# Q and K of a hybrid encoder block: per-head norms taken from the PSUM banks in a written order, eight banks in rotation, K's weight parts prepared under another list of ticks

## The chip, the cores and the metric

One core of one Trainium2 chip. The metric is the device time of one execution in microseconds; the kernel before has a median of 1204.8 us over three runs (1204.0 to 1205.54). All other times here are from one profiled execution of it.

## The reference

One encoder layer on 1024 tokens of width 1024, in float32. What matters here is the projection to Q and K and the norm of each head:

```python
u = rms_norm(x, norm1_g[l])
proj = u @ w_in[l]
q, k, v, cb, cc, ch, ga, gb = jnp.split(proj, split_pts, axis=-1)
q = rms_norm(q.reshape(B, S, N_HEADS, HEAD_DIM), q_norm_g[l])
k = rms_norm(k.reshape(B, S, N_HEADS, HEAD_DIM), k_norm_g[l])
...
y_a = neighbourhood_attention(q, k, v, rpb[l]) @ w_attn_branch[l]
y_b = short_gated_conv(cb, cc, ch, conv_w[l]) @ w_conv_branch[l]
merged = jax.nn.sigmoid(ga) * y_a + jax.nn.sigmoid(gb) * y_b
x = x + merged @ w_o[l]
h = rms_norm(x, norm2_g[l]) @ w_mlp_in[l]
x = x + jnp.square(jax.nn.relu(h)) @ w_mlp_out[l]
```

There are 8 heads of 64, so Q and K are 512 wide each. `rms_norm` divides by the root of the mean square plus 1e-6 and multiplies by a gain.

## The kernel before

Every matmul runs in float16 with both operands split into a high and a low half; three passes (high-high, high-low, low-high) give one product. Splitting is vector work: ScalarE writes the high half, VectorE subtracts it from the float32 value to get the low half. The same is done for the weights, after a scale that comes from the sum of their squares: ScalarE squares the raw weights, TensorE adds over the partitions with a matmul of ones (`all_sum`), VectorE turns the sum into a power of two (`pow2_half`), and then the parts are split. `Chunk.prep` is the generator that emits this for one group of weights.

The tokens are in eight blocks of 128. A unit is one token block against one weight group of 512 columns: 8 slices of the inner dimension by 3 passes, 24 matmuls into one PSUM bank. The stages around the change: V units for blocks 2, 6, 3, 7, 4, 5; eight Q units; eight K units; two units of the first conv group; then the attention stage, in which the conv's other matmuls are mixed with the attention's.

The order of the vector work is set by hand. `fg` and `bg` are lists of generators. `step()` advances all of `fg` by one `yield`, `tick()` the first of `bg`; each call emits a few instructions. `unit(mms, post, steps, ticks)` emits the matmuls, runs the `post` of the unit before (through `settle`), and then interleaves so many steps and ticks. `apart(mark, n)` holds a generator back until n more units have been emitted, and `forced` overrides that. All engines run their instructions in order, so what is emitted earlier on an engine stands in front.

In the Q and K stage each unit's `post` adds a `qk_vec` generator to `fg`: ScalarE copies the bank to `qs` with a scale (L714), squares it (L715); VectorE reduces per head (L718), `rstd` makes the inverse root (VectorE L405, ScalarE's square root L406, VectorE L408 to L414), then VectorE multiplies (L725, for K also the gain, L728), ScalarE makes the high half (L732) and VectorE the low half (L734). `finish_qk` transposes the halves by DMA into `QD` or `KD`. The banks alternate between tag `d` (3 banks) and tag `o` (2 banks).

Beside it run the `sforms`: for four pairs of token blocks, x times its norm (ScalarE L484), four sums on GpSimd (L490), split into halves (ScalarE L504, VectorE L506) and stored to DRAM as `GS` (L511, issued by ScalarE) for a later stage. `xt`, which they read, lies where `QD` is put afterwards. K's weights are prepared by `bg` during the Q units, the first conv group's during the K units. The loop:

```python
for n, (kind, b) in enumerate(todo):
    ch = cQ if kind == "q" else cK
    if n % 8 == 0:
        push(cK if kind == "q" else cConv[0])
    ps = bank("do"[n % 2])
    ...
    unit(tok_mms(ps, actU, b, ch, 8, 512, 0), post, 4, 6 if 4 < n < 8 else 3)
    if n == 3:
        forced[0] = True
        while formed[0] < 4:
            step()
        forced[0] = False
```

Of the kernel before, what the change touches and what calls it, by code (L numbers as in the profile page):

```python
# [10 lines left out]
F32 = mybir.dt.float32  # L11
F16 = mybir.dt.float16
# [40 lines left out]
def encoder_block(ctx: ExitStack, tc: tile.TileContext, x, weights, cols, gqk, rel, masks, out):  # L53
# [22 lines left out]
        return bank("dsodsods"[rc[0] % 8])  # L76


    sc = base.tile([128, 516], F32, name="sc")
    sci = sc.bitcast(I32)  # L80
    area = {"keep": [0, 0, 148], "prep": [148, 148, 244], "tmp": [244, 244, 516]}

    def cols_of(kind, n):
        a = area[kind]
# [6 lines left out]
    def keep(n=1):  # L91
        return cols_of("keep", n)

    def tmp(n=1):
        return cols_of("tmp", n)
# [86 lines left out]
    def apart(mark, n=3, of=units):  # L182
        while of[0] < mark + n and not forced[0]:
            yield WAIT
# [60 lines left out]
    class Chunk:  # L245
# [9 lines left out]
        def prep(self):  # L255
# [5 lines left out]
            if self.kind in "QKCG":  # L261
                self.parts = wsp.tile([128, 2, tot], F16, name="w16_ws", tag="ws")
                for p, (k, w) in enumerate(self.widths):
                    while len(self.raw) <= p:
                        yield WAIT
                    A.activation(self.parts[:, 1, :k * w].bitcast(BF16), self.raw[p][:, :k * w], AF.Square,
                                 accum_out=sc[:, at(rm, p)])
# [4 lines left out]
                V.tensor_tensor(c, sc[:, a], sc[:, gm2], op=OP.mult)  # L272
# [96 lines left out]
    warm = keep()  # L369
    V.memset(sc[:, warm], 1.0)  # L370
    A.activation(sc[:, warm], sc[:, warm], AF.Square)
    minus_half = keep()
    G.memset(sc[:, minus_half], -0.5)
    load_x(0)
    SP.dma_start(sc[:, consts], cols)
# [41 lines left out]
    def rpow(ss, n, y, top):  # L417

        v = tmp()
        G.tensor_scalar(sc[:, v], sc[:, ss], 4.0 ** -top / n, 4.0 ** -top * EPS, op0=OP.mult, op1=OP.add)  # L420
        G.tensor_tensor(sc[:, y], sc[:, v], sc[:, minus_half], op=OP.pow)
        yield

    def pow2_half(ss, top, s, inv, more=0):
# [53 lines left out]
    turned, formed = set(), [0]  # L478
    SFORM = ((9, 0, 0), (9, 2, 1), (10, 1, 0), (10, 3, 1), (11, 0, 1), (12, 1, 1))
# [6 lines left out]
    def sform_sums(n):  # L486
        z = [xt[:, b, c:c + 512] for b in (n, n + 4) for c in (0, 512)]
        for o, a, b, op in ((3, 2, 3, OP.subtract), (2, 0, 2, OP.subtract),
                            (0, 3, 0, OP.subtract), (1, 1, 0, OP.add)):
            G.tensor_tensor(z[o], z[a], z[b], op=op)  # L490

    def sforms():

        for mark, n, split in SFORM:
            yield from apart(mark, 0)
            pair = xt[:, n:n + 5:4]
            if not split:
                sform_rows(n)
                sform_sums(n)
                continue  # L500
            v = wqk.tile([128, 4, 2, 512], F16, name="s16", bufs=3)
            v4 = v.rearrange("p (b h) w c -> p b h w c", b=2)
            f = pair.rearrange("p b (h c) -> p b h c", h=2)
            A.activation(v4[:, :, :, 0], f, AF.Copy)  # L504
            yield
            V.tensor_tensor(v4[:, :, :, 1], f, v4[:, :, :, 0], op=OP.subtract)  # L506
            fg.append(sform_store(n, v))

    def sform_store(n, v):
        yield from apart(units[0], 1)  # L510
        A.dma_start(GS[:, n], v)  # L511
        formed[0] += 1

    def ln_step(b, n=1):
        for _ in range(n):
# [2 lines left out]
    def qk_gain():  # L518
        g = gq[:, 0]
        V.tensor_tensor(g, g, gq[:, 1], op=OP.mult)  # L520
        yield
        yield from gain(g, 11, sgq, isgq)

    def turn_row(b):
        ln_turn(u16[:, ORDER.index(b) % 4], b, UT)
# [164 lines left out]
        ln_step(b, 2)  # L690
        turn_row(b)
    fg.append(qk_gain())
    fg.append(sforms())
    for b in 4, 5:
        v_unit(b, 11)
        step(3)
    settle()
    flush()

    def bias_load(p):  # L700
        t = wbias.tile([128, 2, 3, 128], F32, name="bias")
# [6 lines left out]
        V.scalar_tensor_tensor(te, te, sc[:, cinv], mk[:, 0], op0=OP.mult, op1=OP.add)  # L708
        G.tensor_tensor(m[:, e], te, mk[:, 1], op=OP.add)

    def qk_vec(ps, inv, kind, res):
        qs = wqk.tile([128, 512], F32, name="qs", bufs=3)
        sq = wqk.tile([128, 512], F32, name="sq", bufs=1)
        A.activation(qs, ps, AF.Copy, scale=sc[:, inv])  # L714
        A.activation(sq, qs, AF.Square)  # L715
        yield
        ss, y = tmp(8), tmp(8)
        V.tensor_reduce(sc[:, ss], sq.rearrange("p (h d) -> p h d", h=8), axis=AX, op=OP.add)  # L718
        yield
        yield from rstd(ss, HD, y, 12 if kind == "q" else 0)  # L720
        if kind == "k":
            V.tensor_scalar(sc[:, y], sc[:, y], sc[:, sgq], None, op0=OP.mult)
            yield
        q3 = qs.rearrange("p (h d) -> p h d", h=8)
        V.tensor_tensor(q3, q3, sc[:, y][:, :, None].to_broadcast([128, 8, HD]), op=OP.mult)  # L725
        yield
        if kind == "k":
            V.tensor_tensor(q3, q3, gq[:, 0][:, None, :].to_broadcast([128, 8, HD]), op=OP.mult)  # L728
        r = 2 if kind == "q" else 1
        t = wqk.tile([128, 8, 2, r, HD], F16, name=kind + "16", tag="q16")  # L730
        q4 = q3[:, :, None, :].to_broadcast([128, 8, r, HD])
        A.activation(t[:, :, 0], q4, AF.Copy)  # L732
        yield
        V.tensor_tensor(t[:, :, 1], q4, t[:, :, 0], op=OP.subtract)  # L734
        res.append(t)

    q16 = {}
    todo = [("q", b) for b in ORDER] + [("k", b) for b in range(8)]

    def finish_qk(n):  # L740
        kind, b = todo[n]
        while not q16[n]:
            step()
        dst = QD.rearrange("p a e w t -> p (a e w) t") if kind == "q" else KD
        SP.dma_start_transpose(dst[:, :, b * 128:(b + 1) * 128], q16.pop(n)[0].rearrange("p h w r d -> p (h w r d)"))

    for n, (kind, b) in enumerate(todo):
        ch = cQ if kind == "q" else cK
        if n % 8 == 0:
            push(cK if kind == "q" else cConv[0])  # L750
        ps = bank("do"[n % 2])
        q16[n] = []

        def post(ps=ps, kind=kind, n=n, ch=ch):
            fg.append(qk_vec(ps, ch.inv, kind, q16[n]))
        unit(tok_mms(ps, actU, b, ch, 8, 512, 0), post, 4, 6 if 4 < n < 8 else 3)
        if n == 3:
            forced[0] = True
            while formed[0] < 4:
                step()  # L760
            forced[0] = False
# [8 lines left out]
            SP.dma_start(mk, masks)  # L770
# [4 lines left out]
        if n >= 3:  # L775
            finish_qk(n - 3)
        if n in (5, 6):
            bias_make(*bias[0], n - 5)
        if n % 8 == 7:
            flush()  # L780

# [9 lines left out]

    conv_start(0)
    push(cConv[1])
    first = [bank("o"), bank("o")]
    for half in range(2):
        unit(ch_mms(first[half], actU, half, cConv[0], 8, 384, 0), None, 8, 4)
        finish_qk(13 + half)
    while not q16[15]:
        step()
    settle()  # L800
    finish_qk(15)
    A.activation(sc[:, warm], sc[:, warm], AF.Exp)
    settle()
    drain()
# [1117 lines left out]
```

## Time and profile before

| what | value |
|---|---|
| median of three runs | 1204.8 us |
| the profiled execution | 1205.96 us |
| its span | 1204.2 us |
| TensorE (PE) busy | 1190.9 us, 99% of the span |
| VectorE (DVE) busy | 929.0 us, 77% |
| ScalarE (ACT) busy | 763.3 us, 63% |
| GpSimd (POOL) busy | 435.1 us, 36% |

Times in the views are from the span's start. PEld is TensorE's weight load, which overlaps its matmuls; `ACTq` and `SPq` are the DMA queues that ScalarE and SyncE issue to. The Q units begin at 55.81 us, the K units at 97.28, the conv's first unit at 140.77, and the attention stage at 153.53. Matmuls are pipelined: a unit's matmuls are shown a little longer than the distance from one unit to the next. In brackets stands the idle time ahead of an instruction and what ended it.

### The profile page before, as it was taken

How to read it: one execution, taken by the hardware profiler on the slowest of the kernel's cores; microseconds unless marked ns; L12 is line 12 of the kernel's file. 1: busy time of each engine (PE TensorE's matmuls, PEld its weight loads, DVE VectorE, ACT ScalarE, POOL GpSimd, SP SyncE). 2: the span in 40 equal slices, each digit the busy share in tenths (PEclk: the TensorE clock that was granted, in tenths of full speed). 3: DMA queues.
4: the chain of work that ended last, by engine and by line, in shares of the span. 5: the costliest groups of instructions: out<-in, count | busy, mean ns of one | idle time of the engine just before them, and what ended most of it. 6: DMA issues, size and time to landing. Idle time of an engine off the chain costs nothing.

```text
span 1204.2 us, 16886 instructions
## 1 busy us (share of the span) xinstructions
PE 1190.9 (99%) x6206; PEld 574.7 (48%) x6206; DVE 929.0 (77%) x1721; ACT 763.3 (63%) x1185; POOL 435.1 (36%) x292
## 2 busy tenths in 40 slices
PE   8999999999999999999999999999999999999998
PEld 6444445555444444444468444444444444444444
DVE  6767988988368686877878655545549999999997
ACT  7876679867554555337779778678676744746440
POOL 1641011222311112001004465565567471554662
PEclk9999999999999999999999999999999999999999
DMA  9956746676451211224286545445465926345302
GB/s 284 220 181 139 139 119 134 130 146 120 106 121 68 64 60 52 70 92 188 53 159 185 183 156 192 151 138 193 147 247 201 355 94 223 124 139 194 105 35 105
DMA packets 177250, 174.91 MB, mean 145 GB/s; under 512 B 137744, under 2 KB 138256, under 8 KB 173072
## 3 DMA queue, kind: packets, MB, share of 16 engines
q1 hardware_dynamic: 176592, 169.65, 49.0%
q10 hardware_dynamic: 576, 4.19, 0.8%
q8 instruction: 48, 0.79, 0.3%
q14 instruction: 34, 0.28, 0.1%
HBM read 102.51 MB, written 37.75 MB: 116 GB/s over the span
## 4 chain that ended last, share of the span: by engine, by line
PE 78%; DVE 5%; issue 1%; SPq 1%; ACT 1%; DMA 0%; DVEq 0%; ACTq 0%
PE ps_d L210 28%; PE ps_s L210 24%; PE ps_o L210 17%; PE ps_d L1017 6%; PE ps_o L994 1%; PE ps_s L937 1%; SPq L1088 1%; DVE P L977 1%; DVE w_s L1141 1%; DVE sz L951 1%; DVE sg L1257 0%; DVE w_ws L297 0%; ACT w_s L1145 0%; DMA uT<-gs 0%; DVE sc L317 0%
## 5 line engine op out<-in xcount | busy, mean ns | idle before, releaser
L210 PEld LDWEIGHTS <-ops 128*128 128x128 f16 x1356 | 132.5, 98 | 157.3
L210 PEld LDWEIGHTS <-w 128*128 128x128 f16 x1368 | 132.9, 98 | 139.4
L1017 PE MATMUL ps_d<-uT,w_ws 128*128 128x512 f16 x528 | 123.7, 379 | 0.1
L210 PE MATMUL ps_d<-ops 128*128 128x512 f16 (+1 forms) x528 | 118.3, 374 | 0.0
L1743 ACT ACTIVATE ops<-hf,sc 128x2048 f16<-128x2048 f32 x26 | 52.0, 2000 | 98.2 <-PE ps_o L210 35.5
L210 PE MATMUL ps_s<-ops 128*128 128x512 f16 x492 | 112.9, 379 | 0.0
L1130 POOL TENSOR_TENSOR tsum<-raw 128x512 f32<-128x512 f32 x28 | 46.3, 1668 | 148.8 <-ACT raw L1116 148.7
L1323 POOL TENSOR_TENSOR as<-as 128x512 f32<-128x512 f32 x56 | 77.5, 1385 | 38.9 <-ACT as L1603 35.6
L210 PEld LDWEIGHTS <-w_s 128*128 128x128 f16 x588 | 56.7, 98 | 69.6 <-DVE w_s L1141 1.5
L210 PEld LDWEIGHTS <-uT 128*128 128x128 f16 x528 | 51.4, 98 | 64.0 <-issue 2.3
L210 PE MATMUL ps_d<-u2x,w 128*128 128x512 f16 (+1 forms) x360 | 80.0, 372 | 0.0
L1017 PEld LDWEIGHTS <-w_ws 128*128 128x128 f16 x528 | 51.2, 98 | 54.5 <-DVE cv L839 0.4
L210 PE MATMUL ps_o<-ops 128*128 128x512 f16 x336 | 77.1, 379 | 0.0
L1745 DVE SCALAR_TENSOR_TENSOR ops<-hf,sc,ops 128x2048 f16<-128x2048 f32 x26 | 73.4, 2822 | 4.3 <-ACT ops L1743 4.2
L210 PE MATMUL ps_o<-u2T,w 128*128 128x512 f16 (+1 forms) x324 | 71.7, 371 | 0.0
L1116 ACT ACTIVATE raw<-raw,sc 128x256 f32<-128x256 f32 x172 | 71.0, 494 | 0.9 <-DMA raw<-in_weights 0.9
L1130 POOL TENSOR_TENSOR gsum<-raw 128x512 f32<-128x512 f32 x14 | 19.0, 1377 | 132.3 <-issue 71.3
L1145 ACT ACTIVATE w<-raw,sc 128x512 f16<-128x512 f32 (+1 forms) x28 | 24.6, 927 | 54.0 <-DVE sc L432 54.0
L210 PE MATMUL ps_s<-u2T,w 128*128 128x512 f16 (+1 forms) x252 | 52.7, 359 | 0.0
L1636 DVE TENSOR_TENSOR as<-ps_d,as 128x512 f32<-128x512 f32 (+1 forms) x14 | 9.4, 672 | 55.7 <-ACT as L1655 53.4
L960 ACT ACTIVATE sz<-sz,sc 128x384 f32<-128x384 f32 (+1 forms) x64 | 37.2, 582 | 22.4 <-DVE sc L951 15.0
L306 ACT ACTIVATE w_ws<-raw,sc 128x512 f16<-128x512 f32 (+2 forms) x72 | 40.8, 637 | 14.2 <-DVE sc L279 14.2
(360 smaller groups left out, 2633.5 us busy)
## 6 DMA issues: line engine op xcount, KB each, us to landing
raw<-in_weights SPq DMA_DIRECT2D x88, 512.0 KB, 5.3
hs<-as SPq DMA_DIRECT2D x16, 1792.0 KB, 8.8
hf<-hs SPq DMA_DIRECT2D x26, 1024.0 KB, 7.4
w2x<-in_weights SPq DMA_DIRECT2D x16, 512.0 KB, 8.6
raw<-in_weights SPq DMA_DIRECT2D x16, 384.0 KB, 3.4
xt<-in_x SPq DMA_DIRECT2D x8, 512.0 KB, 8.1
gs<-s ACTq DMA_DIRECT2D x4, 1024.0 KB, 3.9
x<-in_x SPq DMA_DIRECT2D x8, 512.0 KB, 10.1
```

The lines of the kernel that those rows point to most:

```text
L210: T.matmul(ps, l, r, start=a, stop=b)
L306: A.activation(self.parts[:, 0, f + o:f + o + m], self.raw[p][:, o:o + m], AF.Copy, scale=sc[:, c:c + 1])
L937: T.matmul(ps[:, :nb * 128], QD[:, p, e, w, i * 128:(i + 1) * 128], KD[:, 2 * p + e, lo * 128:(lo + nb) * 128], start=w == 0, stop=w == 1)
L951: V.tensor_tensor_reduce(z[:, :d["n"]], d["ps"][:, :d["n"]], bm, sc[:, cneg], 3.0e38, OP.add, OP.min, accum_out=sc[:, d["mx"]])
L960: A.activation(z, z, AF.Exp, scale=-1.0, bias=sc[:, d["mx"]], accum_out=sc[:, d["sm"]])
L1017: T.matmul(ps, l, r, start=a, stop=b)
L1116: A.activation(v, v, AF.Copy, scale=sc[:, at(g, 4 * i + k)])
L1130: G.tensor_tensor(t[:, o], a, b, op=OP.add)
L1145: A.activation(o(0), w, AF.Copy, scale=sc[:, s])
L1323: sub.tensor_tensor(z[o], z[a], z[b], op=op)
L1743: A.activation(P[:, 1, 0], hf, AF.Copy, scale=sc[:, Rs])
L1745: V.scalar_tensor_tensor(P[:, 1, 1], hf, sc[:, Rs], P[:, 1, 0], op0=OP.mult, op1=OP.subtract)
```

## The change

- `qk_vec` and `rstd` are replaced for Q and K by functions that are called in a written order, once per unit (`qk_chain`): square from the bank (ScalarE), the high half of the block before (ScalarE), sum (VectorE), root (ScalarE, with the mean's factor as its scale and a guard for 1e-6 as its bias), the low half of the block before (VectorE), the inverse with one Newton step (four small VectorE operations), and the norm multiply, which reads the bank (VectorE). The copy `qs` out of the bank with its scale is gone; `qk_guard` works the guard out per kind.
- K's multiply of the inverse root by the gain's scale is gone; the gain vector is multiplied once, in `qk_gain`.
- The banks go round all eight, `"dsodsods"[n % 8]`; the second conv half takes an `s` bank.
- The forms are emitted at fixed places instead of by a generator, pairs 2 and 3 and the sums of pair 0 before the Q units, pair 1 at units 0 to 3. Their stores are issued by SyncE instead of ScalarE.
- K's preparation is pushed after unit 0 instead of before it, waits for two units instead of three ahead of its sum, and a list gives the ticks of each unit. The mask and bias loads come at unit 5 instead of 3, the bias steps at units 9 and 10 instead of 5 and 6.
- The halves of a block use buffers of two tags (five buffers in all), the transposes start at unit 4.

```diff
-                yield from apart(units[0], 1 if self.kind == "Q" else 3)
+                yield from apart(units[0], {"Q": 1, "K": 2}.get(self.kind, 3))
...
+    v_unit(4, 11)
+    step(3)
+    sform_rows(0)
+    sform_sums(0)
+    sform_split(2)
+    v_unit(5, 11)
+    step(3)
     settle()
     flush()
+    sform_split(3)
+    sform_store(2)
+    drain()
...
+    def sform_store(n):
+        SP.dma_start(GS[:, n], halves.pop(n))
...
-        A.activation(qs, ps, AF.Copy, scale=sc[:, inv])
-        A.activation(sq, qs, AF.Square)
...
+        A.activation(d["sq"], ps, AF.Square)
...
+        A.activation(sc[:, d["q"]], sc[:, d["ss"]], AF.Sqrt, scale=4.0 ** -TOP[kind] / HD,
+                     bias=sc[:, at(guard[kind], 0)])
...
+        V.reciprocal(sc[:, y], sc[:, q])
+        V.scalar_tensor_tensor(sc[:, q], sc[:, y], -0.5 * 4.0 ** -TOP[kind] / HD, sc[:, y], op0=OP.mult, op1=OP.mult)
+        V.scalar_tensor_tensor(sc[:, q], sc[:, d["ss"]], sc[:, at(guard[kind], 1)], sc[:, q], op0=OP.add, op1=OP.mult)
+        V.scalar_tensor_tensor(sc[:, y], sc[:, q], 1.5, sc[:, y], op0=OP.add, op1=OP.mult)
...
+        V.tensor_tensor(q3, p3, sc[:, d["y"]][:, :, None].to_broadcast([128, 8, HD]), op=OP.mult)
...
+        d["t"] = wqk.tile([128, 8, 2, d["r"], HD], F16, name=todo[n][0] + "16",
+                          **({"tag": "q16"} if n % 5 < 2 else {"tag": "s16", "bufs": 3}))
...
+    def qk_chain(n, ps):
+        qk_square(n, ps)
+        if n:
+            qk_high(n - 1)
+        qk_sum(n)
+        qk_root(n)
+        if n:
+            qk_low(n - 1)
+        qk_inverse(n)
+        qk_norm(n)
+
+    ticks = (0, 2, 4, 4, 6, 6, 6, 6, 2, 2, 3, 4, 4, 5, 5, 1)
+    qk_guard("q", cQ.inv)
     for n, (kind, b) in enumerate(todo):
...
+        if n == 8:
+            push(cConv[0])
+            qk_guard("k", cK.inv)
+        ps = bank("dsodsods"[n % 8])
+        unit(tok_mms(ps, actU, b, cQ if kind == "q" else cK, 8, 512, 0), lambda n=n, ps=ps: qk_chain(n, ps), 0, 0)
+        if n == 0:
+            sform_rows(1)
+            sform_store(3)
+            sform_split(0)
+            sform_sums(1, (0, 1))
+            push(cK)
+        if n == 1:
+            sform_store(0)
+            sform_sums(1, (2, 3))
         if n == 3:
+            sform_split(1)
+        if n == 4:
+            sform_store(1)
...
+        for m in (0, 1, 2) if n == 4 else (n - 2,) if n > 4 else ():
+            qk_turn(m)
+        tick(ticks[n])
+        if n == 5:
+            SP.dma_start(mk, masks)
             bias = {0: bias_load(0)}
+        if n in (9, 10):
+            bias_make(*bias[0], n - 9)
...
-    first = [bank("o"), bank("o")]
+    first = [bank("o"), bank("s")]
     for half in range(2):
         unit(ch_mms(first[half], actU, half, cConv[0], 8, 384, 0), None, 8, 4)
+        if half == 0:
+            qk_high(15)
+            qk_low(15)
+            qk_turn(14)
+            qk_turn(15)
```

More of the change, by code (lines that the diff above doesn't have):

```diff
@@ L371, in encoder_block @@
     A.activation(sc[:, warm], sc[:, warm], AF.Square)
-    minus_half = keep()
+    minus_half = keep(8)
     G.memset(sc[:, minus_half], -0.5)
@@ L522, in qk_gain @@
         yield from gain(g, 11, sgq, isgq)
+        V.tensor_scalar(g, g, sc[:, sgq], None, op0=OP.mult)
+        yield
     def turn_row(b):
@@ L709, in bias_make @@
         G.tensor_tensor(m[:, e], te, mk[:, 1], op=OP.add)
[L711 to L727, printed above, removed]
-            V.tensor_tensor(q3, q3, gq[:, 0][:, None, :].to_broadcast([128, 8, HD]), op=OP.mult)
[L729 to L735, printed above, removed]
@@ L737, in encoder_block, with qk_guard @@
-    q16 = {}
-    todo = [("q", b) for b in ORDER] + [("k", b) for b in range(8)]
-    def finish_qk(n):
+    blocks, guard = {}, {}
+    todo = [("q", b) for b in ORDER] + [("k", b) for b in range(8)]
+    def qk_guard(kind, inv):
+        e, i = keep(2), tmp()
+        V.reciprocal(sc[:, i], sc[:, inv])
+        mul(i, i, i)
+        V.tensor_scalar(sc[:, at(e, 0)], sc[:, i], 4.0 ** -TOP[kind] * EPS, 1e30, op0=OP.mult, op1=OP.min)
+        V.tensor_scalar(sc[:, at(e, 0)], sc[:, at(e, 0)], 1e-30, None, op0=OP.max)
+        V.tensor_scalar(sc[:, at(e, 1)], sc[:, at(e, 0)], 4.0 ** TOP[kind] * HD, None, op0=OP.mult)
+        guard[kind] = e
@@ L747, in encoder_block @@
-    for n, (kind, b) in enumerate(todo):
[L748 to L756, printed above, removed]
+        SP.dma_start_transpose(dst[:, :, b * 128:(b + 1) * 128], blocks.pop(n)["t"].rearrange("p h w r d -> p (h w r d)"))
```

91 lines of the change are left out of this document (43 added, 48 removed).

## The prediction

> **What bounds the kernel now.** I read the page's busy times first, then TensorE's waits over the whole span, then the busy times by stretch, then TensorE's timeline through the Q and K stage.
>
> ```profile
> span 1204.2 us, 16886 instructions
> PE 1190.9 (99%) x6206; PEld 574.7 (48%) x6206; DVE 929.0 (77%) x1721; ACT 763.3 (63%) x1185; POOL 435.1 (36%) x292
> ```
>
> TensorE is the bound: any microsecond has to come out of its gaps. All the waits that it has:
>
> ```profile
> PE ps_o L574 <- DMA xt<-in_x: 4.5, 1, 4.5
> PE ps_d L210 <- DVE w_ws L297: 1.5, 2, 0.9
> PE ps_o L210 <- ACT qs L714: 1.3, 1, 1.3
> PE ps_s L937 <- DVE sc L951: 0.5, 1, 0.5
> PE ps_d L201 <- DVE ones L272: 0.4, 1, 0.4
> ```
>
> The first is the load of x, which the change leaves alone. The second (weights' low halves), third (a bank not yet evicted) and fifth (a sum not ready) lie in the stage that it rewrites. By stretch (PE, then weight loads, DVE, ACT, POOL, granted clock):
>
> ```profile
> 97.00:105.00 8.00, 6.52 (x30) 2.67 (x28) 8.00 (x17) 6.74 (x12) 0.66 (x2) 1.00 0.46 134
> 141.00:154.00 13.00, 11.20 (x53) 4.86 (x52) 11.51 (x33) 8.80 (x19) 0.00 (x0) 1.00 0.79 182
> 154.00:186.00 32.00, 31.86 (x158) 15.17 (x157) 28.03 (x82) 25.35 (x58) 6.08 (x11) 1.00 0.50 119
> ```
>
> The granted clock is 1.00. The gaps stand at 97 to 105 and 141 to 154, where VectorE is 100% and 89% busy: TensorE waits there for vector work that lags. TensorE's timeline (start, duration; a unit is 24 matmuls):
>
> ```profile
> 92.09 5.34 PE L210 MATMUL ps_o<-w_ws,uT 128*128 128x512 f16 x24
> 97.28 0.38 PE L210 MATMUL ps_d<-w_ws,uT 128*128 128x512 f16 x1
> 104.49 5.34 PE L210 MATMUL ps_o<-w_ws,uT 128*128 128x512 f16 x24
> 140.77 5.55 PE L210 MATMUL ps_o<-uT,w_ws 128*128 128x512 f16 x24
> 147.65 5.34 PE L210 MATMUL ps_o<-uT,w_ws 128*128 128x512 f16 x24 [1.33 <-ACT qs L714]
> 153.43 0.16 PE L201 MATMUL ps_d<-ones 128*128 128x1 bf16 x1 [0.44 <-DVE ones L272]
> ```
>
> A unit costs 97.28 - 92.09 = 5.19 us when nothing is late. K's first unit took 104.49 - 97.28 = 7.21 (2.02 lost), the first conv unit 147.65 - 140.77 = 6.88 (1.69 lost), the second 153.43 - 147.65 = 5.78 (0.59 lost). So **4.30 us is the most that this stage can give**; a small further gain is possible where VectorE holds TensorE up in the attention stage behind it.
>
> **The change, part by part.** The durations (busy, mean ns):
>
> ```profile
> L506 DVE TENSOR_TENSOR s<-xt,s 128x2048 f16<-128x2048 f32 x4 | 11.4, 2839 | 8.4 <-ACT s L504 8.4
> L718 DVE TENSOR_REDUCE sc<-sq 128x8 f32<-128x512 f32 x16 | 10.9, 682 | 0.6 <-ACT sq L715 0.6
> L725 DVE TENSOR_TENSOR qs<-qs,sc 128x512 f32<-128x512 f32 x16 | 10.7, 672 | 0.1
> L715 ACT ACTIVATE sq<-qs 128x512 f32<-128x512 f32 x16 | 10.1, 630 | 0.5
> L734 DVE TENSOR_TENSOR q<-qs,q 128x1024 f16<-128x1024 f32 x8 | 9.8, 1223 | 9.1 <-ACT q L732 9.1
> L732 ACT ACTIVATE q<-qs 128x1024 f16<-128x1024 f32 x8 | 8.4, 1053 | 6.1 <-DMA qD<-q 4.1 <-DVE qs L725 2.0
> L714 ACT ACTIVATE qs<-ps_d,sc 128x512 f32<-128x512 f32 x8 | 5.4, 670 | 0.0
> L734 DVE TENSOR_TENSOR k<-qs,k 128x512 f16<-128x512 f32 x8 | 5.5, 690 | 2.0 <-ACT k L732 1.9
> L266 ACT ACTIVATE w_ws<-raw 128x1024 bf16<-128x1024 f32 x4 | 4.2, 1053 | 0.7 <-DVE s L506 0.6
> L266 ACT ACTIVATION_READ_ACCUMULATOR w_ws<-raw 128x1 f32 x12 | 2.2, 187 | 0.0
> L406 ACT ACTIVATE sc<-sc 128x8 f32<-128x8 f32 x16 | 3.3, 208 | 13.0 <-DVE sc L405 12.9
> L410 DVE SCALAR_TENSOR_TENSOR sc<-sc 128x8 f32<-128x8 f32 x16 | 2.6, 163 | 0.2
> L537 DVE SCALAR_TENSOR_TENSOR vT<-ps_d,vT 128x512 f16<-128x512 f32 x1 | 0.7, 674 | 0.0
> L708 DVE SCALAR_TENSOR_TENSOR bias<-bias,sc,mk 128x384 f32<-128x384 f32 x2 | 1.2, 606 | 0.0
> L830 DVE TENSOR_TENSOR z<-ps_d,z 128x512 f32<-128x512 f32 x4 | 2.7, 687 | 0.3 <-PE ps_d L1017 0.3
> ```
>
> *Removed:* the copy out of the bank, 16 x 0.67 = 10.7 us of ScalarE; on VectorE the pre-scale of each root and K's extra multiply by the gain. *Changed:* the norm multiply reads the bank. Out of SBUF it took 672 ns, a multiply of the same shape out of a bank (L830) 687: 15 ns x 16 = 0.2 us. The Trainium skill speaks against this edit: VectorE: DVE Perf Modes, Rules for kernel authors, advises to accept the slow rate on matmul output or to copy it to SBUF first if many operations follow. Its errata section puts a bank source 62 cycles (some 65 ns) above SBUF, by which the six norms ahead of K's weights would cost 0.4 us where the rows give 0.1; the rows above disagree, and I go by them. *Added:* five small guard operations per kind, about 0.2 us each when each waits for the last: 1.0 us twice.
>
> *Banks.* Each block's bank was reused after four or six units; with eight in rotation it is after eight, over 40 us. The 1.69 us at the first conv unit goes (its second half now takes an `s` bank that K1 left long before); nothing else there is late, if the low halves of its weights are in time (below).
>
> *K's weights* are what decides. Counting the steps of the preparation against the new tick list, its sum's matmul is still issued in Q unit 4, its scales in unit 5 and its parts in unit 6, as before; what changes is what stands ahead of them on VectorE. There I write the new order down from the trace's own starting points:
>
> ```profile
> 59.29 3.02 DVE L506 TENSOR_TENSOR s<-xt,s 128x2048 f16<-128x2048 f32 x1 [2.38 <-ACT s L504]
> 64.81 1.91 ACT L504 ACTIVATE s<-xt 128x2048 f16<-128x2048 f32 x1 [0.72 <-POOL xt L490]
> 87.50 1.23 DVE L734 TENSOR_TENSOR q<-qs,q 128x1024 f16<-128x1024 f32 x1 [0.81 <-ACT q L732]
> 91.35 1.23 DVE L734 TENSOR_TENSOR q<-qs,q 128x1024 f16<-128x1024 f32 x1 [0.74 <-ACT q L732]
> 97.22 0.67 DVE L718 TENSOR_REDUCE sc<-sq 128x8 f32<-128x512 f32 x1
> 51.12 5.39 DVE L297 SCALAR_TENSOR_TENSOR w_ws<-raw,sc,w_ws 128x512 f16<-128x512 f32 x8 [0.79 <-ACT w_ws L306]
> ```
>
> One Q chain on VectorE is sum 0.60 (0.68 less overlap), low 1.15, inverse 0.85 (four dependent small ones), norm 0.60: 3.2 us, or up to 3.75 where it also waits for ScalarE's high (1.05). The old order took 91.35 - 87.50 = 3.85. VectorE's ends, in us from the span's start:
> - split 2: 62.3 (59.29 + 3.02). Low halves of V4 and V5 (some 0.6 each) and the gain's small ones: 64.2.
> - split 3 (2.84): 67.1; guard: 68.1; split 0, whose high half ends at 66.7 as POOL frees it in the trace: 70.9.
> - chain 0 (nothing before it to overlap): 73.4.
> - chain 1, behind two squares of K's raw weights on ScalarE (2 x 1.24 with the read-out): 78.7; chain 2, behind the other two: 83.1.
> - split 1, with POOL quiet: 85.6. Chain 3: 88.8; two small ones: 89.0; chain 4: 92.6; K's six scale operations: 93.8; chain 5: 97.0.
> - first low half of K (5.39 / 8 = 0.67): **97.7**. K0's first matmul needs only a high half and starts at 97.28; the second waits for this one, some 0.3 us. After that a low half comes every 0.67 us, and three matmuls (0.65) use one. **K0 loses 0.3 to 0.4 instead of 2.02: a gain of 1.7.**
>
> The stall that goes in the old order is that VectorE stood at a reduction, and K's parts behind it, at 97.2; next late is the same queue, 0.3 us behind TensorE.
>
> *Then to the conv.* VectorE ends the eight low halves at 102.4; with K chains of 3.25 (sum, low, inverse, norm, gain) against units of 5.19, two bias steps (0.6) and the second guard, it ends chain 12 at about 127.8, before K5's bank is full (97.6 + 6 x 5.19 = 128.7). It has caught up; chain 14 ends at 137.9, the first conv low half at 139.3. TensorE comes to the conv at 97.6 + 8 x 5.19 = 139.1 and needs that half from its third matmul (139.5). No loss at the conv; the eight banks cover the lag of up to 12 us in between. At the end of the second unit (149.5) the conv-1 sum is needed; chain 15, its high and low, then reduce and multiply end at about 149.8: 0.3 to 0.4 lost, as 0.59 was. So the sum's matmul stands at 149.9 instead of 153.43: **3.5 us earlier**.
>
> *Moved at the same time:* four stores of forms, from ACT's queue to SP's. Ahead of them lie only loads already due; behind them the transposes, which need the same VectorE work anyway, and the bias load, used 20 us later.
>
> ```profile
> gs<-s ACTq DMA_DIRECT2D x4, 1024.0 KB, 3.9
> DMA to landing us min/median/max: 4.2/4.3/7.2
> ```
>
> The store of pair 1 frees the buffer of block 4's halves: 85.6 + 3.9 = 89.5 against 92.6, when they are wanted; with the longest landing of the transposes (second line, for qD) 92.8, a cost of 0.2.
>
> *Behind it.* The attention stage has VectorE at 28.03 of 32 us. VectorE ended the K tail at 155.4 (the row below); in the list above it does so at about 149.8 and has only the conv-1 scales left then. That is 5 us earlier, more than TensorE's 3.5, so its work moves with TensorE's and is some 1.5 further ahead. Of the hole there (0.5 at L937 in the waits) I count 0.2; bounds 0 and 0.5.
>
> ```profile
> 154.67 0.69 DVE L734 TENSOR_TENSOR k<-qs,k 128x512 f16<-128x512 f32 x1 [0.69 <-ACT k L732]
> ```
>
> **Sum:** 1.7 + 1.7 + 0.1 + 0.2 = 3.7. The profiled execution took 1205.96 us (span 1204.2), so it would be 1202.3; the median of the three runs, 1204.8, lies 1.2 below that execution, so **1201.1**.
>
> **The rivals.**
> - *Part of the gain is not collected* (0.22). Either the queue ahead of K's weights is 1 to 3 us longer than in my list (splits at 3.02 instead of 2.84, chains at the old 3.85), or the attention stage's VectorE, 88% busy, hands some of the 3.5 back. That K's parts are issued in the same unit as before speaks for it. With chains 1 to 5 at 3.85 and slow splits K's first low half comes at about 100.1: gain 1.3, 1203.5.
> - *The chain does not overlap* (0.14). In the written order VectorE meets ScalarE three times per block (square, root, high), each in order. If nothing overlaps, a block takes 0.63 + 0.68 + 0.21 + 1.05 + 1.22 + 0.85 + 0.67 = 5.3, less the square, which the banks take ahead: 4.7. Five such chains add 5 x 1.1 = 5.5: K's first low half at 103.2, 1206.6. It makes the kernel slower from about 4.3 us a block on. Against it: low stands between sum and inverse, so the root's hand-over is covered; the old order, with the same meetings, took 3.85.
> - *All of it goes*, with the hole behind it: 4.3 + 0.5 = 4.8, 1200.0. That is the end of the forecast's range, not a case of its own.
>
> **How the numbers follow.** A measurement of this kernel tells about 0.2% (2.4 us) from no change. The forecast, with 0.64, lies from 1199.5 (all of it, and 0.5 for the runs' own spread, 1204.0 to 1205.5) to 1202.4, all faster. The first rival is within 0.2%. Of the second's 0.14, 0.05 lie within 0.2% (as its 1206.6 does) and 0.09, with a late store or landing on top, above 1207.2. So faster 0.64, same 0.27, slower 0.09. The range goes from 1199.5 to 1205.0, which holds the first rival; the second is left out.
>
> **What would show it.** Right: no TensorE wait on ACT at the first conv unit; a K0 unit of 5.5 to 5.6 us; the conv-1 sum's matmul near 149.9; ScalarE 10 us less busy; the norm multiply out of a bank near 690 ns. Wrong: K0 over 7 us with VectorE in chain 5 at its start (the queue is longer than listed); a TensorE wait on `ones` at unit 4 (K's sum late); the gap at 185 grown (given back); ScalarE's high waiting for a store. If VectorE idles over 1 us a block ahead of its low halves, the forecast is wrong by its main term.

## The result and the profile after

The kernel after has a median of 1199.68 us over six runs (1199.03 to 1200.83), the kernel before 1204.95 over six (1204.0 to 1205.66): a ratio of 0.9958, 95% interval 0.9945 to 0.9971, so between 3.5 and 6.6 us are gone. The profiled execution of the kernel after took 1199.51 us. Its page:

```profile
span 1197.7 us, 16871 instructions
PE 1188.3 (99%) x6206; PEld 573.6 (48%) x6206; DVE 939.3 (78%) x1708; ACT 753.0 (63%) x1169; POOL 432.9 (36%) x292
```

ScalarE has 10.3 us less to do, VectorE is busy 10.3 us longer. All of TensorE's waits after (total, times, longest):

```profile
PE ps_o L565 <- DMA xt<-in_x: 4.6, 1, 4.6
PE ps_s L980 <- DVE sc L994: 0.5, 1, 0.5
PE ps_s L210 <- DVE w_s L1184: 0.3, 1, 0.3
PE ps_d L210 <- DVE w_s L1184: 0.2, 1, 0.2
```

Of the five quoted before, the load of x stays, and so does the 0.5 us that was at L937 and is now at L980; the three of the Q and K stage are gone. (The kernel before has three more waits, which the prediction's list of all waits lacks: 0.6 us for raw weights, 0.3 for `uT<-gs`, 0.2 for `w_s`. They lie outside the stage.) TensorE's timeline after (start, duration; the units are Q7, K0, K1, the two of the conv, and the conv-1 sum):

```profile
89.98 5.34 PE L210 MATMUL ps_s<-w_ws,uT 128*128 128x512 f16 x24
95.16 5.49 PE L210 MATMUL ps_d<-w_ws,uT 128*128 128x512 f16 x24
100.48 5.34 PE L210 MATMUL ps_s<-w_ws,uT 128*128 128x512 f16 x24
...
136.84 5.58 PE L210 MATMUL ps_o<-uT,w_ws 128*128 128x512 f16 x24
142.25 5.34 PE L210 MATMUL ps_s<-uT,w_ws 128*128 128x512 f16 x24
147.43 0.17 PE L201 MATMUL ps_d<-ones 128*128 128x1 bf16 x1
```

Where a span's difference lies is read best from stretches that begin and end at the same matmul in both kernels. The busy times by stretch of before (length; PE, weight loads, DVE, ACT, POOL; clock; DMA share and GB/s), cut at the first Q unit, the first K unit, the conv-1 sum and the last pair of matmuls of Q by K:

```profile
0.00:55.81 55.81, 50.72 (x227) 30.86 (x228) 37.87 (x80) 43.43 (x81) 22.54 (x32) 1.00 0.95 247
55.81:97.28 41.47, 41.47 (x195) 18.80 (x194) 29.18 (x64) 31.20 (x42) 17.96 (x9) 1.00 0.60 188
97.28:153.43 56.15, 52.87 (x242) 23.36 (x241) 46.81 (x136) 37.57 (x73) 1.93 (x1) 1.00 0.66 135
153.43:287.90 134.47, 133.84 (x999) 69.21 (x998) 120.10 (x363) 107.59 (x255) 30.77 (x44) 1.00 0.62 128
287.90:1204.20 916.30, 912.04 (x4548) 432.47 (x4546) 694.99 (x1084) 543.50 (x737) 361.87 (x206) 1.00 0.44 140
```

and of after, cut at the same matmuls:

```profile
0.00:53.69 53.69, 49.12 (x227) 29.82 (x228) 37.75 (x79) 42.94 (x81) 22.55 (x32) 1.00 0.98 254
53.69:95.16 41.47, 41.47 (x195) 18.80 (x194) 36.48 (x73) 30.35 (x42) 16.05 (x8) 1.00 0.58 179
95.16:147.43 52.27, 52.22 (x242) 23.27 (x241) 47.07 (x114) 30.17 (x60) 1.96 (x4) 1.00 0.72 156
147.43:281.36 133.93, 133.45 (x999) 69.31 (x998) 119.86 (x361) 105.88 (x254) 30.39 (x42) 1.00 0.63 128
281.36:1197.70 916.34, 912.06 (x4548) 432.38 (x4546) 698.10 (x1084) 543.65 (x737) 361.92 (x206) 1.00 0.44 140
```

The 6.5 us between the spans are 2.12 ahead of the first Q unit, 0 in the Q units, 3.88 from the first K unit to the conv-1 sum, and 0.54 in the attention stage; all the rest took 0.04 longer. The first 2.12 are not put down to the change: 2.11 of them are there by the first V unit already (24.70 and 22.59 us), ahead of where the order of the work was changed, and the first Q unit begins anywhere from 53.38 to 55.81 us in the 14 profiles of this study, 53.38 to 55.10 in the seven built from the kernel after and 53.55 to 55.81 in the seven built from the kernel before (54.2 and 54.3 on average). The profile of before is the latest of all. So **the change itself is worth 3.9 us in its stage and 0.5 behind it, 4.4 in all**, which lies within the timed 3.5 to 6.6.

The second rows show how. TensorE's 41.47 us of Q units are the same in both, but VectorE has done 36.48 us of work in them instead of 29.18: its idle time there is 5.0 instead of 12.3. So VectorE is further ahead when the K units begin; how little of the gain needs that lead is shown by b_all below. VectorE's groups after, and ScalarE's, from 55 to 155 us:

```profile
L498 DVE TENSOR_TENSOR s<-xt,s 128x2048 f16<-128x2048 f32 x4 | 11.2, 2800 | 2.2 <-ACT s L497 2.2
L764 DVE TENSOR_TENSOR q<-qs,q 128x1024 f16<-128x1024 f32 x8 | 9.8, 1220 | 1.4 <-ACT q L760 1.4
L751 DVE TENSOR_TENSOR qs<-ps_s,sc 128x512 f32<-128x512 f32 x6 | 4.1, 692 | 0.2
L726 ACT ACTIVATE sq<-ps_s 128x512 f32<-128x512 f32 x6 | 3.5, 576 | 0.0
L736 ACT ACTIVATE sc<-sc 128x8 f32<-128x8 f32 x16 | 4.8, 298 | 10.2 <-DVE sc L731 10.2
```

The large instructions of VectorE take what they took, and it has no less to do: from the first Q unit to the sum it is busy 83.55 us instead of 75.99. What went is its idle time ahead of the forms' low halves (8.4 us before at L506, 2.2 now) and ahead of Q's low halves (9.1 before at L734, 1.4 now), both spent waiting for ScalarE's high halves.

### The profile page after: what moved, and what is told of

The parts are those of the page before. It is cut to its first block, busy times and chain, and to the rows that moved or that the text cites. A ratio compares the mean times of both kernels' runs of the same rounds, so it can differ in the third digit from the quotient of the medians.

```text
span 1197.7 us, 16871 instructions
## 1 busy us (share of the span) xinstructions
PE 1188.3 (99%) x6206; PEld 573.6 (48%) x6206; DVE 939.3 (78%) x1708; ACT 753.0 (63%) x1169; POOL 432.9 (36%) x292
## 4 chain that ended last, share of the span: by engine, by line
PE 79%; DVE 13%; ACT 5%; issue 2%; DMA 0%; POOL 0%; DVEq 0%; ACTq 0%
PE ps_d L210 27%; PE ps_s L210 24%; PE ps_o L210 17%; PE ps_d L1060 8%; DVE w_s L1184 2%; PE ps_s L980 1%; PE ps_o L1037 1%; DVE s L498 1%; DVE sg L1300 1%; ACT w_ws L266 1%; DVE w_ws L297 1%; DVE q L764 1%; DVE qs L751 1%; ACT sq L439 1%; ACT w_ws L306 1%
## 5 line engine op out<-in xcount | busy, mean ns | idle before, releaser
L1786 ACT ACTIVATE ops<-hf,sc 128x2048 f16<-128x2048 f32 x26 | 52.0, 2000 | 97.7 <-PE ps_o L210 35.2
```

The costliest lines, as they stand in the source:

```text
L1786: A.activation(P[:, 1, 0], hf, AF.Copy, scale=sc[:, Rs])
```

## The experiments

Two theories were tried. **Theory 1**, the prediction's: three separate holes (late weight parts at K0, a bank at the conv, the conv-1 sum), each closed by its own edit, and the gains add up. **Theory 2**: one queue, VectorE's with ScalarE's, paces everything from K0 to the sum, and a hole that one edit closes opens again at the next place where TensorE meets that queue. A name that begins with `b_` is built from the kernel before, with `a_` from the kernel after. "Stage" is the time from the first Q matmul to the conv-1 sum's matmul, 97.62 us before and 93.74 after; two executions of the kernel after differ in it by 0.15 (93.59 in a second one).

### K's parts alone: b_parts

```diff
-        unit(..., post, 4, 6 if 4 < n < 8 else 3)
+        if n == 6:
+            unit(..., post)
+            tick(6)
+            step(4)
+        else:
+            unit(..., post, 4, 6 if 4 < n < 8 else 3)
```

> The kernel before, with one edit: in Q unit 6 the six ticks (K's weight parts) are emitted ahead of the four steps instead of between them. Theory 1 (three separate holes): K0 loses 0 to 0.3 us instead of 2.02 and nothing else changes: 2.0 us faster than before. Theory 2 (one vector queue paces the whole stage up to the attention): K0's hole closes too, but VectorE's and ScalarE's work ends no earlier, so TensorE meets the wait again at the first conv unit and at the sum's matmul, which stays within 0.6 us of 153.4: 0 to 0.6 us faster.

Measured: 1202.44 against 1204.87 us (ratio 0.9981, 0.9972 to 0.999); stage 95.77, so 1.85 shorter. TensorE's timeline of it at K0, K1, the second conv unit and the sum:

```profile
96.37 5.34 PE L210 MATMUL ps_d<-w_ws,uT 128*128 128x512 f16 x24
101.55 5.34 PE L210 MATMUL ps_o<-w_ws,uT 128*128 128x512 f16 x24
...
144.90 5.34 PE L210 MATMUL ps_o<-uT,w_ws 128*128 128x512 f16 x24 [1.33 <-ACT qs L714]
150.67 0.16 PE L201 MATMUL ps_d<-ones 128*128 128x1 bf16 x1 [0.44 <-DVE ones L272]
```

K0 loses nothing, and the other two holes stand as they stood (1.33 and 0.44, as before). Theory 2's forecast, 0 to 0.6 us, fails here. The 2.02 us at K0 was a hole of its own: an order of two calls closes it, and the vector work that is pushed back has time to catch up over the eight K units.

### The banks alone: b_banks

```diff
-        ps = bank("do"[n % 2])
+        ps = bank("dsodsods"[n % 8])
...
-    first = [bank("o"), bank("o")]
+    first = [bank("o"), bank("s")]
```

> The kernel before, with the eight-bank rotation for the Q and K units and an s bank for the second conv half, nothing else. Theory 1: the 1.33 us wait on ScalarE at the second conv unit goes: 1.3 to 1.7 us faster. Theory 2: the wait goes, but the conv-1 sum's matmul still waits for VectorE until about 153.2 on a span like the one before, with a wait there of some 1.5 us instead of 0.44: 0 to 0.3 us faster.

Measured: 1205.19 against 1204.87 (1.0004, 0.9995 to 1.0013); stage 97.58. TensorE's timeline at the second conv unit and the sum:

```profile
144.25 5.34 PE L210 MATMUL ps_s<-uT,w_ws 128*128 128x512 f16 x24
151.53 0.16 PE L201 MATMUL ps_d<-ones 128*128 128x1 bf16 x1 [1.93 <-DVE ones L272]
```

The wait for the bank is gone and the wait for the sum has grown from 0.44 to 1.93 us: what is won at the bank is given back one unit later, to the same queue. Theory 1 fails here, theory 2 holds.

### Both together: b_both

The two edits above in one kernel.

> The kernel before, with both edits (ticks ahead of steps in Q unit 6, and eight banks). Theory 1: the terms add: 3.4 to 3.7 us faster, most of the change's gain without touching the norm. Theory 2: 0.3 to 1 us faster, the rest is lost waiting for VectorE at the conv's weights and the conv-1 sum.

Measured: 1201.82 against 1204.87 (0.9981, 0.9972 to 0.999); stage 95.82, against 95.77 for the parts alone. With K0's hole closed the banks are still worth nothing, and the sum is late by the same 1.93 us. So neither theory holds whole: K0's hole stands by itself, the bank's and the sum's are one.

### The old banks in the kernel after: a_oldbanks

The edit of b_banks, the other way round, in the kernel after.

> The changed kernel with the banks as before (d and o in turn, two o banks for the conv). Theory 1: only the second conv unit meets a bank that is not free: K7's norm multiply ends at about 143.8 in the changed kernel, the unit would start at 142.25, so 1.6 us slower than the changed kernel. Rival: since the bank is now held until the norm multiply and VectorE is up to 11 us behind, Q and K units wait too: over 3 us slower, with waits on DVE at several units.

Measured: 1201.58 against 1204.87 (0.9974, 0.9964 to 0.9983); stage 95.25, 1.5 longer than after. TensorE's timeline at the second conv unit and the sum:

```profile
144.54 5.35 PE L210 MATMUL ps_o<-uT,w_ws 128*128 128x512 f16 x24 [1.49 <-ACT w_ws L266]
149.73 0.17 PE L201 MATMUL ps_d<-ones 128*128 128x1 bf16 x1
```

So in the kernel after the same edit is worth 1.5 us. The name in the bracket is a ScalarE instruction that came last by the profile; the matmul goes into the `o` bank that K7 used, and with two such banks in turn it has to wait for K7's norm multiply, which ends at 144.48 by VectorE's timeline. The banks pay once the vector work behind the last K unit ends early enough to be ready at the sum. Which part of the change makes it end early was the next question.

### More buffers for the halves: b_bufs

```diff
-        t = wqk.tile([128, 8, 2, r, HD], F16, name=kind + "16", tag="q16")
+        t = wqk.tile([128, 8, 2, r, HD], F16, name=kind + "16",
+                     **({"tag": "q16"} if n % 5 < 2 else {"tag": "s16", "bufs": 3}))
```

on top of b_both.

> The kernel before with eight banks and the ticks ahead of the steps in Q unit 6, and besides the halves of a block in five buffers (two tags) instead of two. What is left there is one wait of 1.9 us at the conv-1 sum, 1.8 us behind the changed kernel. Theory A (the queue is late because ScalarE's high half waited 4.1 us for a transpose to free its buffer): the wait goes or falls under 0.5, the sum's matmul comes some 94 us after Q0's start instead of 95.8: 1.4 to 1.9 us faster than those two edits alone, 3.5 us faster than before. Theory B (the order of the tail, conv parts mixed with the last blocks' steps) and theory C (the copy out of the bank): VectorE has caught up by then anyway, 0 to 0.4 us.

Measured: 1201.95 against 1204.83 (0.9977, 0.9968 to 0.9986); stage 94.71, 1.1 shorter than b_both, while the times of the two can't be told apart. Its wait for the sum:

```profile
PE ps_d L201 <- DVE ones L272: 1.3, 1, 1.3
```

ScalarE's wait for the transposes out of the halves' buffers (4.1 us before, 1.5 in b_both) is gone, and the sum comes 1.1 us earlier: 0.4 of it in the first conv unit (5.18 us instead of 5.61 in b_both), 0.7 in the wait shown.

### The conv's parts in one piece: b_tail

```diff
-        if n % 8 == 7:
+        if n == 15:
+            forced[0] = True
+            while bg:
+                tick()
+            forced[0] = False
+        elif n % 8 == 7:
             flush()
```

on top of b_both.

> The kernel before with eight banks and the ticks ahead of the steps in Q unit 6, and besides the conv weights' parts behind K unit 7 emitted in one piece, ahead of the last two blocks' steps, instead of mixed with them. Theory B: the conv unit's 0.2 us wait goes and the tail ends earlier since no block's step stands between two parts: 0.8 to 1.9 us off the 1.9 us wait at the conv-1 sum. Theories A and C: the same work in another order, the sum is ready at the same time or later: 0 to 0.3 us.

Measured: 1202.12 against 1204.83 (0.9982, 0.9972 to 0.9991); stage 95.90. Its wait for the sum:

```profile
PE ps_d L201 <- DVE ones L272: 2.4, 1, 2.4
```

The 0.4 us lost in the first conv unit (5.61 us in b_both, 5.18 here) went and came back at the sum (2.4 instead of 1.9). Without the buffers it is worth nothing. Behind this wait TensorE's granted clock, the last number but two of this row, stood at half:

```profile
150.10:151.00 0.90, 0.90 (x5) 0.32 (x3) 0.20 (x2) 0.76 (x2) 0.13 (x2) 0.50 0.84 152
```

The next seven matmuls took 2.95 us there instead of the 1.67 that they take elsewhere, and the attention stage behind it is 1.0 longer than in b_both. Behind the waits of 1.93 us the clock stayed at 1.00 in the profiles of b_banks and b_both.

### Both of these: b_all

The kernel before with the parts, the banks, the buffers and the conv's parts in one piece, but with the copy and the generators of the old order.

> The kernel before with all four edits: eight banks, ticks ahead in Q unit 6, five buffers, conv parts in one piece; norm, copy, stores and forms as before. If order and buffers made the gain, the sum's matmul comes 93.7 to 94.2 us after Q0's start and the kernel is within 0.5 us of the changed one. If the copy's removal is needed (theory C), the wait at the conv-1 sum stays over 1 us and it is 1.3 to 1.9 us slower than the changed kernel.

Measured: 1202.01 against 1204.83 (0.9978, 0.9968 to 0.9988); stage 94.00, only 0.26 longer than after. Its waits in and behind the stage:

```profile
PE ps_d L210 <- DMA uT<-gs: 1.2, 1, 1.2
PE ps_d L201 <- DVE ones L272: 0.5, 1, 0.5
```

Its busy times in the Q units (order as above):

```profile
54.52:95.99 41.47, 41.47 (x194) 18.81 (x193) 28.92 (x62) 30.65 (x42) 16.93 (x9) 1.00 0.60 192
```

By its stage, the old vector order, copy and all, reaches nearly what the written order reaches, once K's parts, the banks, the buffers and the conv's parts are changed: 3.6 of the 3.9 us. It does so without the lead: VectorE has done 28.92 us of work in the Q units, no more than before. So neither the early forms nor the norm out of the bank is needed for most of the stage's gain.

By its time it does not reach it: its interval (0.9968 to 0.9988) and that of the kernel after (0.9945 to 0.9971) hardly touch. From the first Q unit on, its profile is 1.9 us longer than that of after: 0.3 in the stage, 0.5 in the attention stage (134.45 against 133.93), and 1.1 in the last part (917.4 against 916.3), where a transfer comes late at 343 us (1.23 us at `uT<-gs`, which was 0.28 before and 0 after, and between 0 and 1.23 over all profiles). That last part took 915.6 to 917.5 us over the 14 profiles, 917.0 in a second one of the kernel after, so one profile doesn't tell whether the edits have to do with it. That stays open.

### The copy back in the kernel after: a_copy

```diff
-        A.activation(d["sq"], ps, AF.Square)
+        d["ps"] = wqk.tile([128, 512], F32, name="qs", bufs=3)
+        A.activation(d["ps"], ps, AF.Copy)
+        A.activation(d["sq"], d["ps"], AF.Square)
...
-        qs = wqk.tile([128, 512], F32, name="qs", bufs=2)
+        qs = d["ps"]
```

> The changed kernel with the copy out of the bank put back on ScalarE (0.58 us a block, 16 blocks); square and norm read the copy. Theory C (the copy's removal is needed): chains 1 and 2, where ScalarE is the later engine, end 0.6 us later each, K's first low half 0.6 to 1.2 us later, so K0 loses some 1 us, and the tail another 0.3 to 0.6: 0.8 to 1.6 us slower than the changed kernel. Theories A and B (order and buffers): ScalarE has room, 0 to 0.4 us.

Measured: 1202.05 against 1204.83 (0.9977, 0.9968 to 0.9986); stage 96.01, 2.3 longer than after. TensorE's waits in the stage:

```profile
PE ps_d L210 <- DVE w_ws L297: 1.2, 1, 1.2
PE ps_o L210 <- ACT w_ws L306: 0.5, 1, 0.5
```

Groups of it, from 55 to 155 us:

```profile
L753 DVE TENSOR_TENSOR qs<-qs,sc 128x512 f32<-128x512 f32 x16 | 11.1, 692 | 0.5
L733 DVE TENSOR_REDUCE sc<-sq 128x8 f32<-128x512 f32 x16 | 10.9, 680 | 2.5 <-ACT sq L728 2.4
L728 ACT ACTIVATE sq<-qs 128x512 f32<-128x512 f32 x16 | 10.1, 630 | 0.5
L727 ACT ACTIVATE qs<-ps_s 128x512 f32<-128x512 f32 x6 | 3.5, 577 | 0.0
```

Per block ScalarE has 577 + 630 - 576 ns more, so 0.63 us, and in a written order that stands ahead of VectorE's sum: VectorE waits 2.4 us for the squares, where it waited 0.2 after, and K's first low halves come too late for K0, which takes 6.61 us instead of 5.32. The other 1.0 us is lost at the conv and its sum. In this order the copy costs; in the old order, where b_all has it, it hid. The same view holds a second answer: the norm multiply out of SBUF takes 692 ns here, out of a bank 692 after. Here the bank costs VectorE nothing.

### The queue delayed on purpose: a_delay

```diff
+        if n == 6:
+            w = wqk.tile([128, 512], F32, name="sq", bufs=2)
+            for _ in range(3):
+                V.tensor_copy(w, blocks[5]["ps"])
         tick(ticks[n])
```

> The changed kernel with three copies of a bank to SBUF on VectorE (about 0.65 us each, 1.9 in all) put between chain 5 and K's weight parts; their result is not used. K's first low half then comes 1.9 us later. The prediction's view (VectorE runs just ahead of TensorE at K0): K0 loses 1.7 to 2.0 us instead of 0.14, and since nothing behind it waits, the kernel is 1.7 to 2.0 us slower than the changed one. Rival (K0 has slack, or the loss is absorbed by the holes at the conv): under 1 us.

Measured: 1201.51 against 1205.08 (0.9971, 0.996 to 0.9981; the kernel after, timed again beside it as a_again, 1200.17, 0.9958, 0.9946 to 0.9971); stage 95.80, 2.2 longer than the 93.59 of a_again. TensorE's waits in the stage, in full:

```profile
PE ps_d L210 <- DVE w_ws L297: 1.9, 1, 1.9
```

The three added copies take 2.13 us by VectorE's timeline, and 1.9 to 2.2 come out at TensorE. So K's weights have no slack in the kernel after, and within the stage what is lost there doesn't come back. This rests on the profile: by the medians a_delay is 1.3 us slower, less than expected, and the two intervals overlap.

> The changed kernel, unchanged, timed again. Its profile shows 3.9 us gained from Q0's start to the conv-1 sum and 0.5 behind it; the other 2.1 us of the two profiles' difference lie ahead of Q0, where the instructions are the same. If those are the spread of the first loads' landing, Q0 starts at 53.4 to 55.8 us here too and the gain over the kernel before is 4.0 to 5.3 us. If the change does something to the start, Q0 starts within 0.2 us of 53.7 again and the gain is above 5.3.

Measured: the time given above, 4.9 us less than the kernel before, so under 5.3. The first Q unit began at 53.81 us, which lies within both of the ranges that were set for it and decides nothing by itself; the starts of the two sets of seven profiles, given with the result, speak for spread.

### One tick moved: a_rows

```diff
-    ticks = (0, 2, 4, 4, 6, 6, 6, 6, 2, 2, 3, 4, 4, 5, 5, 1)
+    ticks = (0, 2, 4, 4, 6, 6, 6, 6, 2, 2, 3, 4, 4, 5, 6, 0)
```

> The changed kernel with the last tick of the conv weights' scales one unit earlier (unit 14 instead of 15), so that ScalarE can make the conv's high halves while VectorE still works on block 14. The conv's first unit took 5.41 us and started 0.07 late; if that is the wait for those scales, 0.2 to 0.3 us faster than the changed kernel. If VectorE's low halves bind it, 0.

Measured: 1200.45 against 1205.08 (0.9958, 0.9946 to 0.9971); stage 93.29. TensorE's timeline at the conv:

```profile
138.03 5.34 PE L210 MATMUL ps_o<-uT,w_ws 128*128 128x512 f16 x24
143.21 5.34 PE L210 MATMUL ps_s<-uT,w_ws 128*128 128x512 f16 x24
148.39 0.17 PE L201 MATMUL ps_d<-ones 128*128 128x1 bf16 x1
```

Each of the units takes 5.18 us: the last 0.3 us of the stage are closed, and with them all of the 4.3 that the prediction counted in it (97.62 - 93.29). In the timed runs nothing is seen of it (1200.45 against 1200.17 for a_again on the same chip, ranges of 2.3 us each).

### The stores on ScalarE's queue again: a_store

```diff
-        SP.dma_start(GS[:, n], halves.pop(n))
+        A.dma_start(GS[:, n], halves.pop(n))
```

on top of a_rows.

> The changed kernel with the conv scales one unit earlier, and the four stores of forms issued from ScalarE's queue again, at the same places of the order. The prediction counted their move at nothing. If that holds, the sum's matmul stays 93.2 to 93.6 us after Q0's start and the time within 0.3 us of the kernel with the scales alone. If not, ScalarE, which now has to wait for VectorE's split ahead of each store before it may go on to the chain's square and root, delays chains 0 and 3 by 1 to 3 us and K0 waits: 1 to 3 us slower.

Measured: 1199.87 against 1204.84 (0.9958, 0.9944 to 0.9971); stage 93.71. ScalarE's waits beside the stores:

```profile
ACT s L497 <- DVE sc L713: 2.4, 1, 2.4
ACT xt L482 <- DVE s L498: 0.7, 1, 0.7
```

On ScalarE's queue a store has to wait for VectorE's low half, and ScalarE stands behind it. The stage is 0.4 longer than a_rows, all of it in K0 (5.60 us instead of 5.18), which waits for K's low halves; in time the two can't be told apart. SyncE's queue is the better place, for at most 0.4 us.

## Why the prediction was right, and where it was off

**The total.** 1201.1 was forecast and 1199.68 came, within the range of 1199.5 to 1205.0 but only 0.2 us from its lower end. The sum of the terms was 3.7; the two profiles show 4.4 (1.9, 1.4, 0.6 and 0.5, below). The medians differ by 5.3 here and by 4.9 beside a_again; the runs' own spread doesn't allow more than "3.5 to 6.6". Where the 0.5 to 0.9 us between the profiles and the medians lie is open.

**K's weights, the main term: 1.9 instead of 1.7.** K0 was to lose 0.3 to 0.4 us and lost 0.14 (100.48 - 95.16 = 5.32 against 5.18), in a_again nothing. The list of VectorE's ends was to put K's first low half at 97.7. To compare, 2.12 us are added to the times of after, whose Q units begin that much earlier: it ended at 97.5 (the eight begin at 94.62, the first ends at 95.36). The list was wrong in its middle and right at its end. The guard and the first chain beside GpSimd took longer than the 1.0 and 2.5 us that it gives them (1.8 and 3.5), so the norm of chain 0 ended at 75.5 and not 73.4. Chains 1 and 2 took 2.0 us of it back, at 3.9 us each instead of the 5.3 and 4.4 that it puts down for their place behind the squares of K's raw weights. That the two errors cancel is luck. That there is no cover behind this list, as the prediction said ("0.3 us behind TensorE"), a_delay shows.

**The banks: 1.4 instead of 1.7, and earned under a condition.** 1.69 us were to go because the second conv unit takes a bank that K1 left long before, with no loss at the conv. They did go but for 0.3 (142.25 - 136.84 = 5.41, so 0.23 are left, and 0.07 ahead of the unit), which a_rows closes; without the banks 1.5 come back (a_oldbanks). But the eight banks alone are worth 0 (b_banks) and 0 with K's parts in time (b_both): the same queue is then late at the sum. The prediction did follow that queue to the sum, 0.3 us late there, so in its own order the addition holds. What it doesn't say is that the term hangs on that end of the queue: with the end 2.1 us later, as in b_both (95.82 against 93.74), the whole term is gone.

**The conv-1 sum: 0.6 instead of 0.1.** A loss of 0.3 to 0.4 was to remain of the 0.59, which by itself makes 0.2 to 0.3 and not the 0.1 that was added up. None does (147.43 - 142.25 = 5.18): the reduce and multiply behind VectorE's tail were to end at 149.8 and ended at 149.4 with the 2.12 added, so `ones` was ready 0.1 us ahead of TensorE. VectorE's timeline after:

```profile
146.35 0.69 DVE L764 TENSOR_TENSOR k<-qs,k 128x512 f16<-128x512 f32 x1 [1.65 <-ACT k L760]
147.15 0.16 DVE L272 TENSOR_TENSOR ones<-sc 128x1 bf16<-128x1 f32 x1
```

So the sum's matmul came 3.88 us earlier from the first Q unit, against 3.5 forecast. That the tail is early enough is the work of the buffers and of the conv's parts in one piece (1.1 and a further 0.7 us from b_both to b_all), neither of which had a term in the prediction; the last 0.3 us came with the rest of the change.

**The attention stage: 0.5 instead of 0.2, and in another place.** 0.2 was counted for the 0.5 us hole at L937. That hole didn't move (0.5 at L980 after, and in every kernel of the study). The stage is 0.54 shorter all the same, most of it because of two gaps of about 0.2 us that no wait names: at 184 us before, a pair of matmuls at 184.42 is followed 0.46 us later by the next, after by 0.22 (178.13 to 178.35), and likewise at 164. All seven kernels built from after have 133.9 to 134.0 us here, all but one built from before 134.5 (b_tail 135.4). It fits the prediction's remark that VectorE would be further ahead of TensorE there; it wasn't tried apart.

**The rivals.** *Part is not collected*: the queue ahead of K's weights wasn't longer at its end, and nothing is seen to be handed back behind the stage (0.04 us over the last 916). *The chain does not overlap* was to cost 4.7 us a block: the norms of chains 0 to 2 end 3.9 us apart. Its mechanism is real, though: a_copy shows that 0.63 us more of ScalarE per block, in this order, already costs 2.3. *All of it goes* is nearly what the stage did (3.9 of 4.3, and 4.3 in a_rows).

**The smaller steps.** ScalarE was to lose 10.7 us of work and lost 10.3. No wait of TensorE for ScalarE is left at the conv, as said. VectorE was to have caught up by chain 12, 0.9 us before K5's bank is full. It had not: chain 12 ends with this multiply by the gain, at 127.97, 1.6 us behind the end of K5's unit (126.4):

```profile
127.28 0.69 DVE L753 TENSOR_TENSOR qs<-qs,gq 128x512 f32<-128x512 f32 x1
```

A chain of K takes VectorE 3.6 us here (119.33 to 122.94 from one norm multiply to the next) instead of the 3.25 put down for it. It caught up at chain 14, early enough for the conv. The norm multiply was to take about 690 ns and takes 691 to 692, but not because of the bank: a_copy has 692 out of SBUF. The rule of the Trainium skill that was weighed (VectorE: DVE Perf Modes, Rules for kernel authors and the errata section, with 62 cycles more for a bank) is not borne out by this pair. The errata section of that page of the Trainium skill also gives 691 ns for a float32 addition of two tensors 512 wide; that agrees with both.

## What to carry to other kernels

A gap in the engine that bounds the kernel is worth its size only if the queue that ends it is early at the next place where the two meet: before adding up gaps, follow each to its queue, and count those of one queue as one where it can't catch up between them. A hole at freshly prepared weights can be a matter of two calls in the wrong order, so try the order alone first; it held 1.9 of the 4.4 us here. Four edits of order, banks and buffers gave 3.6 of the 3.9 us of the stage without the new norm, so try such edits before rewriting the work itself. Compare two profiles stage by stage between the same matmuls, not span by span: here a third of the difference of the spans lay ahead of where the order was changed.

## What the runs showed of the hardware

**VectorE's small operations beside GpSimd.** VectorE's timeline after, while GpSimd's additions ran, and just behind them:

```profile
65.39 1.03 DVE L102 TENSOR_TENSOR sc<-sc 128x1 f32<-128x1 f32 x1
71.31 1.12 DVE L744 SCALAR_TENSOR_TENSOR sc<-sc 128x8 f32<-128x8 f32 x1
76.09 0.23 DVE L744 SCALAR_TENSOR_TENSOR sc<-sc 128x8 f32<-128x8 f32 x1
```

and GpSimd's timeline:

```profile
55.89 16.52 POOL L489 TENSOR_TENSOR xt<-xt 128x512 f32<-128x512 f32 x8 [7.76 <-ACT xt L482]
```

The same instruction takes 1.12 us while GpSimd works and 0.23 once it is done; the first ends at 72.43, GpSimd's last addition at 72.41. The Trainium skill (SBUF — State Buffer, SBUF: two separate sides) says that a VectorE operation with two SBUF inputs and a GpSimd operation that reads SBUF shut each other out for a whole instruction, not for a share of the rate. These rows agree; the prediction had given such operations 0.2 us throughout.

**ScalarE out of a bank.** A square out of a bank took 576 ns, out of SBUF 630: taking ScalarE's copy away also made the square cheaper. A root with its bias from a tile took 298 ns where one without took 208. The Trainium skill (ScalarE: Activation LUTs, What ACT_TABLE_LOAD costs) gives some 93 ns for such an operand; 90 agrees.

**TensorE's clock behind a wait.** In b_tail TensorE waited 2.44 us, and behind it the granted clock was 0.50 for some 3 us and then 1.00 again; behind waits of 1.93 us (b_banks, b_both) it was 1.00. One profile shows it, and why the clock fell stays open.
